# First block's attention: turning, copying and value products one step later, with a fourth buffer for the probabilities

## The chip, the cores and the metric

The kernel runs on one core of a Trainium2 chip. The time is device microseconds (us) of one launch. Five engines work beside each other, each through its own list of instructions in order: TensorE (PE; PEld is its weight load), VectorE (DVE), ScalarE (ACT), GpSimd (POOL) and SyncE (SP, which issues DMAs).

## The reference, cut to what matters

The program is a long chain: two layers of a first block (attention, a gated convolution network, an mLSTM layer, another network), then a second block. The change is in the attention of the first block's layer 0. There 768 tokens (512 of the sequence, 256 of a context) go through two attentions of 8 heads, and each is this:

```
def attend(q, k, v):                      # blocks of 128 queries
    s = einsum('bqgrd,bsgd->bgrqs', qi, k).astype(float32) * scale
    p = softmax(s, axis=-1)
    return einsum('bgrqs,bsgd->bqgrd', p, v)
...
ka, va = concatenate([ka_c, ka_l]), concatenate([va_c, va_l])   # context, sequence
out_lat = merge(attend(mla_q(...), ka, va), attend(gqa_q(...), kb, vb))
out_ctx = merge(attend(mla_q(ctx), ka_c, va_c), attend(gqa_q(ctx), kb_c, vb_c))
```

A block of sequence queries sees 768 keys; a block of context queries sees the 256 context keys. GQA has 8 query heads on 2 key heads; MLA has 8 heads of width 96.

## The kernel before, in words

All of it is written in fp32 with the operands of a large product split in a high and a low part (fp32r), so scores take two (GQA) or three (MLA) products.

`run()` inside `attn()` does an attention, once for GQA (178 to 283 us of the profile) and once for MLA (333 to 460 us). It cuts the work into 48 units: one head and one block t of 128 queries; t = 0 to 3 are of the sequence (768 keys wide), t = 4 and 5 of the context (256 wide). In MLA the units of a head follow each other (t0 to t5); in GQA two heads alternate, so twelve units make a group.

A unit goes through steps, each on one engine:

- `S`: scores, PE, into a double bank D of PSUM (two buffers).
- `X`: DVE finds the row maximum (L1938) and the bias (L1939); ACT writes exp and its row sum (L1942) into a buffer of the tag "ca" (three).
- `R`: DVE reciprocal (L1946), then POOL multiplies the probabilities (L1947).
- `Tr`: PE turns 128x128 pieces (L1958) into banks A (two buffers, columns up to 512) and B (one buffer, the last 256).
- `CpB` (ACT, L1963) and `CpA` (DVE, L1968): copies to SBUF, into one tile pT (four buffers).
- `PV`: at every odd unit PE multiplies the values with the pT of a pair of units (L1980: 24 matmuls, or 8 where the pair is 256 wide), into bank V (one buffer).
- `EvH` (ACT, L1995) and `EvL` (DVE, L2000): the high and low part of the output leave V.
- `preT`, `preH`, `preL`: the next head's queries and keys are turned on PE (three parts in MLA: two into a bank A at t0 and t1, the third into the D bank of unit t4), then split by ACT (L2014) and DVE (L2021).

`pipeline` sets the order. In round u it calls every step for unit u minus its lag, in the order of the list, and each engine executes what it is given in that order:

```
for u in range(n + max(l for l, _ in stages)):
    for lag, f in stages:
        if 0 <= u - lag < n:
            f(u - lag)
```

So one round is, on PE: S(u+1), preT(u), Tr(u-2), PV(u-4). On ACT: preH(u-1), CpB(u-3), exp(u), EvH(u-5). On DVE: maximum and bias (u), reciprocal (u-1), EvL(u-6), CpA(u-3), preL(u-1). On POOL: the product of u-1. Nothing is loaded from memory in either stage; a tail (`tail`) fills the rounds after the last unit.

A buffer that is taken again makes its first writer wait for its last reader. That is how an order on one engine becomes a wait on another.

Of the kernel before, what the change touches and what calls it, by code (L numbers as in the profile page):

```python
# [12 lines left out]
F32 = mybir.dt.float32  # L13
# [7 lines left out]
P = 128  # L21
# [4 lines left out]
TT = T + TC  # L26
# [155 lines left out]
class Kernel:  # L182
# [1503 lines left out]
    def attn(self):  # L1686
# [16 lines left out]
        esT, pT = self.pool("attT", "left")  # L1703
# [208 lines left out]
        def run(by_head, prep, scores, value, sc, out, bg, tail):  # L1912
# [4 lines left out]
            esW, pW = self.pool(self.nm("attW"), "left")  # L1917
            units = ([(h + c, t) for h in (0, 2, 4, 6) for t in range(6) for c in range(2)] if by_head else
                     [(h, t) for h in range(8) for t in range(6)])
            U = [dict(W=768 if t < 4 else 256) for h, t in units]  # L1920

            def S(u):
                h, t = units[u]
                d = U[u]
                d["s"] = b = self.bank("D").rearrange("p a b -> p (a b)")
                if t == 4 and h + by_head < 7:
                    U[u - 1]["pre"] = prep(h + 1 + by_head, 2, b[:, 0:512])
                if d["W"] == 768:
                    scores(h, t, b, 0, 512)
                scores(h, t, b, 512, 768)  # L1930

            def X(u):
                h, t = units[u]
                d = U[u]
                s = d.pop("s")[:, 768 - d["W"]:768]
                scale = sc[:, t, h:h + 1]
                mx, b = self.tmp(2, tag="mx", bufs=3), self.tmp(2, tag="mb", bufs=3)
                nc.vector.tensor_reduce(mx[:, 0:1], s, AX.X, ALU.max)  # L1938
                nc.vector.scalar_tensor_tensor(b[:, 0:1], mx[:, 0:1], -1.0, scale, ALU.mult, ALU.mult)  # L1939
                d["e"] = e = self.tmp(TT, tag="ca", bufs=3)[:, :d["W"]]  # L1940
                d["z"] = z = self.tmp(2, tag="z", bufs=6)
                nc.scalar.activation(e, s, AF.Exp, bias=b[:, 0:1], scale=scale, accum_out=z[:, 0:1])  # L1942

# [15 lines left out]

            def CpB(u):  # L1960
                d = U[u]
                d["p"] = p = pW.tile([P, TT], F32, tag="pT", bufs=4, name=self.nm("pT"))
                nc.scalar.activation(p[:, T:], d.pop("B")[:, :TC], AF.Copy)  # L1963

            def CpA(u):
# [57 lines left out]
            for i in range(6 if by_head else 3):  # L2023
                U[0]["pre"] = prep(i // 3, i % 3, self.bank("AAVBAA"[i]))
                preH(0)
                preL(0)
            S(0)
            self.pipeline(len(units), ((1, preH), (3, CpB), (0, X), (1, R), (6, EvL), (5, EvH), (3, CpA), (1, preL),
                                       (0, bg), (-1, S), (0, preT), (2, Tr), (4, PV)), tail)
            esW.close()  # L2030
            self.psum()

        def split_tile(pool, **kw):
            o = pool.tile([P, 2, 4, TT], F32R, name=self.nm("o"), **kw)
            return o[:, 0], o[:, 1]

        self.oG = split_tile(pO, tag="o")
        run(True, prep_g, scores_g, lambda h, j: G2[:, j, 128 + h // 4 * 64:192 + h // 4 * 64], scG, self.oG,
            kv_norm, lambda i: lat_q(i) if i < 2 else None)
        esg.close()  # L2040
# [87 lines left out]
        def tail(i):  # L2128
            if i == 0:
                self.ao_start()  # L2130
            if i < 4:
                self.ao_fm(self.ao0, self.w0, i)
        run(False, prep_m, scores_m, lambda h, j: V[:, j, h], scM,
            self.oM, lambda u: None, tail)
        esm.close()
# [639 lines left out]
```

## Time and profile before

| what | before |
|---|---|
| median of 3 runs | 3823.54 us (3820.2 to 3829.47) |
| profiled execution | 3818.78 us, of which 3817.0 us is its span |
| PE busy in the span | 3619.6 us, 95% |
| DVE, ACT, POOL busy | 67%, 42%, 19% |
| PE busy 178 to 286 us (GQA) | 95.85 of 108.00 us, granted clock 0.95 |
| PE busy 336 to 462 us (MLA) | 116.76 of 126.00 us, granted clock 0.96 |

The page gives averages over a program of many stages; the two stages here are 6% of the span, so they are read by themselves: PE's list in order of time, and what it waited for.

### The profile page before, as it was taken

To read this page: it belongs to the slowest core of one execution; us is meant where nothing else is said; L and a number is where in the kernel's file an instruction comes from. 1 tells how busy PE (TensorE), PEld (TensorE's weight loads), DVE (VectorE), ACT (ScalarE), POOL (GpSimd) and SP (SyncE) were. 2 spreads that over 40 slices of the span, in tenths; PEclk is the share of its full clock that TensorE was granted. 3 is DMA by queue.
4 is the path that set the end of the run, shared out by engine and by line. 5 is a ranking of instruction groups with operands and counts; after the bars stand their busy time and mean duration, and the time that the engine had idled before them with its cause. 6 is when DMAs were issued, how large, how long until landed. Compare 5 with 4: busy or idle time off the path is not lost. (4 is left out here: it accounts for less than half of the span.)

```text
span 3817.0 us, 54418 instructions
## 1 busy us (share of the span) xinstructions
PE 3619.6 (95%) x21148; PEld 3100.9 (81%) x21148; DVE 2564.8 (67%) x4103; ACT 1594.1 (42%) x2678; POOL 722.6 (19%) x755
## 2 busy tenths in 40 slices
PE   7988999999999989999999998999999999899999
PEld 5877788888887778877789876788878898678997
DVE  7977687665645285444577768677765777766776
ACT  2365632122235294332344446444444444464443
POOL 6334230010021193000100025000030000550000
PEclk8999999999999999999999998999999999899999
DMA  5300043343423542323233322333234332213332
GB/s 178 108 2 23 27 126 118 118 130 112 128 63 100 156 122 73 102 84 100 77 99 108 96 66 82 92 100 100 82 120 126 93 106 85 82 48 105 92 108 73
DMA packets 570400, 363.48 MB, mean 95 GB/s; under 512 B 17719, under 2 KB 546605, under 8 KB 570141
## 3 DMA queue, kind: packets, MB, share of 16 engines
q1 hardware_dynamic: 564317, 346.21, 31.1%
q0 software_dynamic: 3520, 9.59, 0.8%
q8 instruction: 167, 2.74, 0.3%
q10 hardware_dynamic: 2304, 4.20, 0.3%
q14 instruction: 92, 0.75, 0.1%
HBM read 345.72 MB, written 14.20 MB: 94 GB/s over the span
## 5 line engine op out<-in xcount | busy, mean ns | idle before, releaser
L135 DVE TENSOR_TENSOR wl<-ws,wh 128x1024 fp32r<-128x1024 f32 (+3 forms) x474 | 584.7, 1243 | 314.6 <-ACT wh L132 312.0
L132 ACT ACTIVATE wh<-ws 128x1024 fp32r<-128x1024 f32 (+3 forms) x474 | 457.6, 978 | 586.9 <-DVE ws L454 257.2
L562 PE MATMUL D<-ah,wl 128*128 128x256 f32 x1344 | 380.3, 283 | 11.0 <-DVE wl L135 11.0
L560 PE MATMUL D<-ah,wh 128*128 128x256 f32 x1344 | 377.1, 281 | 1.7 <-DVE gu L602 1.7
L561 PE MATMUL D<-al,wh 128*128 128x256 f32 x1344 | 376.5, 280 | 0.9 <-DVE al L495 0.9
L539 PE MATMUL M<-hz,wh 128*128 128x512 f32 x704 | 279.9, 398 | 2.3 <-DVE xT L545 2.3
L540 PE MATMUL M<-hz,wh 128*128 128x512 f32 x704 | 280.4, 398 | 1.0 <-DVE hz L638 0.9
L541 PE MATMUL M<-hz,wl 128*128 128x512 f32 x704 | 278.7, 396 | 0.0
L341 POOL TENSOR_TENSOR acc<-acc,t 128x512 f32<-128x512 f32 x36 | 46.8, 1301 | 1171.5 <-ACT t L340 1171.5
L562 PEld LDWEIGHTS D<-ah,wl 128*128 128x128 f32 x1344 | 252.7, 188 | 18.3 <-DVE wl L135 18.3
L560 PEld LDWEIGHTS D<-ah,wh 128*128 128x128 f32 x1344 | 252.8, 188 | 6.1 <-ACT wh L132 2.4
L561 PEld LDWEIGHTS D<-al,wh 128*128 128x128 f32 x1344 | 252.8, 188 | 5.0 <-DVE al L495 1.3
L321 PE MATMUL D<-ah,wl 128*128 128x512 f32 (+1 forms) x616 | 242.7, 394 | 6.5 <-DVE wl L135 6.5
L317 PE MATMUL D<-ah,wh 128*128 128x512 f32 (+1 forms) x616 | 244.7, 397 | 3.0 <-ACT wh L132 2.7
L319 PE MATMUL D<-al,wh 128*128 128x512 f32 (+1 forms) x616 | 242.8, 394 | 0.8 <-POOL al L2697 0.4
L303 POOL TENSOR_TENSOR hl<-t,hh 128x768 fp32r<-128x768 f32 (+1 forms) x44 | 69.9, 1588 | 796.4 <-ACT hh L302 735.9
L1349 DVE SCALAR_TENSOR_TENSOR as<-ws,S,as 128x256 f32<-128x256 f32 x448 | 202.8, 504 | 3.6 <-DMA ws<-in_ada_w_dram 0.2
L560 PE MATMUL E<-ah,wh 128*128 128x256 f32 x672 | 188.9, 281 | 6.8 <-ACT t L590 4.0
L562 PE MATMUL E<-ah,wl 128*128 128x256 f32 x672 | 189.9, 283 | 4.7 <-DVE wl L135 4.7
L561 PE MATMUL E<-al,wh 128*128 128x256 f32 x672 | 188.1, 280 | 0.0
L317 PE MATMUL D<-x7h,wh 128*128 128x512 f32 (+1 forms) x464 | 183.7, 399 | 2.6 <-ACT x7h L2692 1.6
L319 PE MATMUL D<-x7l,wh 128*128 128x512 f32 (+1 forms) x464 | 181.6, 394 | 0.6 <-DVE x7l L2699 0.6
(711 smaller groups left out, 9550.2 us busy)
## 6 DMA issues: line engine op xcount, KB each, us to landing
ws<-in_ffn_w_up_dram SPq DMA_DIRECT2D x104, 512.0 KB
ws<-in_ada_w_dram SPq DMA_DIRECT2D x88, 512.0 KB
t<-in_ffn_w_down_dram SPq DMA_DIRECT2D x128, 256.0 KB
ws<-in_ffn_w_gate_dram SPq DMA_DIRECT2D x88, 256.0 KB
ws<-in_ffn_w_up_dram SPq DMA_DIRECT2D x88, 256.0 KB
wz<-in_ffn_w_gate_dram SPq DMA_DIRECT2D x56, 256.0 KB
wz<-in_ffn_w_up_dram SPq DMA_DIRECT2D x56, 256.0 KB
ws<-in_ffn_w_down_dram SPq DMA_DIRECT2D x32, 384.0 KB
```

Of the source, the lines that this page charges most:

```text
L132: self.nc.scalar.activation(h[:, :n], t[:, :n], AF.Copy)
L135: self.nc.vector.tensor_tensor(l[:, :n], t[:, :n], h[:, :n], ALU.subtract)
L317: nc.tensor.matmul(o, wh[:, kw + k], xh[:, k0 + k, s], start=a, stop=False)
L319: nc.tensor.matmul(o, wh[:, kw + k], xl[:, k0 + k, s], start=False, stop=False)
L321: nc.tensor.matmul(o, wl[:, kw + k], xh[:, k0 + k, s], start=False, stop=z)
L539: nc.tensor.matmul(q, wh[:, k], h[:, 0, i], start=a, stop=False)
L540: nc.tensor.matmul(q, wh[:, k], h[:, 1, i], start=False, stop=False)
L541: nc.tensor.matmul(q, wl[:, k], h[:, 0, i], start=False, stop=z)
L560: nc.tensor.matmul(o, wh[:, u, k], xh(k0 + k, s), start=start and k == 0, stop=False, skip_group_check=True)
L561: nc.tensor.matmul(o, wh[:, u, k], xl(k0 + k, s), start=False, stop=False, skip_group_check=True)
L562: nc.tensor.matmul(o, wl[:, u, k], xh(k0 + k, s), start=False, stop=stop and k == 3, skip_group_check=True)
L1349: nc.vector.scalar_tensor_tensor(t, w[:, kk], c, t, ALU.mult, ALU.add)
```

## The change

The steps Tr, CpA, CpB, PV, EvH and EvL move one round later against S, X, R and the pre steps. The exp of every fourth unit goes to a buffer of its own in the stage's pool, so four units of probabilities can be held; the tiles pT go from four to three, so the SBUF used is the same.

```diff
-                d["e"] = e = self.tmp(TT, tag="ca", bufs=3)[:, :d["W"]]
+                e = (pW.tile([P, TT], F32, tag="e", name=self.nm("e")) if u % 4 == 3 else
+                     self.tmp(TT, tag="ca", bufs=3))
+                d["e"] = e = e[:, :d["W"]]
...
-                d["p"] = p = pW.tile([P, TT], F32, tag="pT", bufs=4, name=self.nm("pT"))
+                d["p"] = p = pW.tile([P, TT], F32, tag="pT", bufs=3, name=self.nm("pT"))
...
-            self.pipeline(len(units), ((1, preH), (3, CpB), (0, X), (1, R), (6, EvL), (5, EvH), (3, CpA), (1, preL),
-                                       (0, bg), (-1, S), (0, preT), (2, Tr), (4, PV)), tail)
+            self.pipeline(len(units), ((1, preH), (4, CpB), (0, X), (1, R), (7, EvL), (6, EvH), (4, CpA), (1, preL),
+                                       (0, bg), (-1, S), (0, preT), (3, Tr), (5, PV)), tail)
```

Lines after the new ones stand three lower in the changed kernel (L1942 becomes L1945, L1995 becomes L1998, L2014 becomes L2017). No instruction is added or removed on any engine, and the lists of the rest of the program are as before.

ACT's list in the MLA stage, rounds t2 to t5 of one head, before (mqh: the high part of the next head's queries and keys; pT<-B: a copy; t<-D: an exp; o<-V: an output):

```order
L1963 ACTIVATE pT_4347<-B_4330 128x256
L1942 ACTIVATE t_4353,t_4354<-D_4318,t_4350,scM 128x768
L1995 ACTIVATE o_3229<-V_4333 64x128 x2
L1963 ACTIVATE pT_4376<-B_4373 128x256
L1942 ACTIVATE t_4382,t_4383<-D_4361,t_4379,scM 128x768
L2014 ACTIVATE mqh_4294<-D_4390 96x2x256
L1963 ACTIVATE pT_4412<-B_4403 128x256
L1942 ACTIVATE t_4418,t_4419<-D_4390,t_4415,scM 128x256
L1995 ACTIVATE o_3229<-V_4406 64x128 x2
```

The same engine and rounds in the changed kernel:

```order
L1966 ACTIVATE pT_4536<-B_4532 128x256
L1945 ACTIVATE t_4542,t_4543<-D_4520,t_4539,scM 128x768
L1966 ACTIVATE pT_4573<-B_4557 128x256
L1945 ACTIVATE e_4579,t_4580<-D_4550,t_4576,scM 128x768
L1998 ACTIVATE o_3229<-V_4560 64x128 x2
L2017 ACTIVATE mqh_4477<-D_4586 96x2x256
L1966 ACTIVATE pT_4603<-B_4599 128x256
L1945 ACTIVATE t_4609,t_4610<-D_4586,t_4606,scM 128x256
```

EvH (o<-V) has moved from even rounds (after the exps of t2 and t4) to odd ones, and now stands between the exp of t3 and preH of the next head (mqh<-D).

DVE's list in the same stage, round t4 of one head, before (mql: the low part; D: a row maximum out of the scores):

```order
L1938 TENSOR_REDUCE t_4205<-D_4181 128x1
L1939 SCALAR_TENSOR_TENSOR t_4206<-t_4205,scM 128x1
L1946 RECIPROCAL t_4174<-t_4174 128x1
L1968 COPY pT_4203<-A_4189 128x512
L2021 TENSOR_TENSOR mql_4086<-D_4181,mqh_4085 96x2x256
```

And in the changed kernel:

```order
L1938 TENSOR_REDUCE t_4187<-D_4168 128x1
L1939 SCALAR_TENSOR_TENSOR t_4188<-t_4187,scM 128x1
L1949 RECIPROCAL t_4162<-t_4162 128x1
L2003 TENSOR_TENSOR o_3229<-V_4142,o_3229 64x128 x2
L1971 COPY pT_4185<-A_4176 128x512
L2024 TENSOR_TENSOR mql_4060<-D_4168,mqh_4059 96x2x256
```

EvL (o<-V,o) has moved into the rounds of even units, here between the reciprocal and the copy that stand ahead of the next head's preL (mql<-D).

## Rows read from the trace of the kernel before

**Rows 1.** Timeline of PE, one MLA head: start, duration, instruction, [idle before <- releaser].

```profile
400.72 1.53 PE L1980 MATMUL V<-pT,mv 128*64 128x128 f32 x24
402.18 0.50 PE L1908 MATMUL D<-mqh 96*128 96x512 f32 x1
...
403.34 0.60 PE L1958 MATMUL A<-ident,t 128*128 128x128 f32 x4
...
404.00 0.38 PE L1901 MATMUL D<-ident,mq 128*96 128x128 f32 x2
...
404.79 0.60 PE L1958 MATMUL A<-ident,t 128*128 128x128 f32 x4
...
405.54 0.66 PE L1980 MATMUL V<-pT,mv 128*64 128x128 f32 x8
406.13 0.39 PE L1908 MATMUL D<-mqh 96*128 96x256 f32 x1
...
407.03 0.38 PE L1958 MATMUL B<-ident,t 128*128 128x128 f32 x2
408.53 0.50 PE L1908 MATMUL D<-mqh 96*128 96x512 f32 x1 [1.11 <-DVE mql L2021]
```

**Rows 2.** Timeline of DVE in the same rounds.

```profile
403.54 0.96 DVE L1938 TENSOR_REDUCE t<-D 128x1 f32<-128x768 f32 x1 [0.80 <-PE D L1910]
...
404.80 0.59 DVE L2000 TENSOR_TENSOR o<-V,o 64x128 fp32r<-64x128 f32 x2
405.42 0.69 DVE L1968 COPY pT<-A 128x512 f32<-128x512 f32 x1
406.38 0.42 DVE L1938 TENSOR_REDUCE t<-D 128x1 f32<-128x256 f32 x1 [0.27 <-ACT mqh L2014]
...
406.99 0.67 DVE L1968 COPY pT<-A 128x512 f32<-128x512 f32 x1
407.78 0.69 DVE L2021 TENSOR_TENSOR mql<-D,mqh 96x512 fp32r<-96x512 f32 x1
```

**Rows 3.** Timeline of ACT in the same rounds.

```profile
404.79 0.99 ACT L1942 ACTIVATE t<-D,t,scM 128x768 f32<-128x768 f32 x1
...
405.77 0.58 ACT L2014 ACTIVATE mqh<-D 96x512 fp32r<-96x512 f32 x1
```

**Rows 4.** Waits, 349 to 463 us (MLA): us in total, times, longest.

```profile
PE D L1908 <- DVE mql L2021: 6.7, 6, 1.1
PEld A L1958 <- POOL t L1947: 0.7, 1, 0.7
```

**Rows 5.** Waits, 188.3 to 283.4 us (GQA).

```profile
PEld D L1888 <- ACT t L1942: 4.3, 11, 1.0
PE B L1958 <- ACT pT L1963: 2.4, 3, 0.9
PE A L1958 <- POOL t L1947: 1.7, 1, 1.7
```

**Rows 6.** Timeline of PE in GQA: one round, and a group's first scores twice.

```profile
216.06 0.50 PE L1888 MATMUL D<-gkh,qs 128*128 128x512 f32 x1
...
216.86 0.60 PE L1958 MATMUL A<-ident,t 128*128 128x128 f32 x4
...
217.61 1.53 PE L1980 MATMUL V<-pT,rawG 128*64 128x128 f32 x24
...
229.89 0.50 PE L1888 MATMUL D<-gkh,qs 128*128 128x512 f32 x1 [0.49 <-ACT t L1942]
...
254.90 0.48 PE L1888 MATMUL D<-gkh,qs 128*128 128x512 f32 x1
```

**Rows 7.** Timeline, end of MLA: an output that waits for its value product.

```profile
452.37 1.53 PE L1980 MATMUL V<-pT,mv 128*64 128x128 f32 x24
...
453.95 0.56 ACT L1995 ACTIVATE o<-V 64x128 fp32r<-64x128 f32 x2 [1.02 <-PE V L1980]
```

**Rows 8.** Busy us and counts by stretch: PE, PEld, DVE, ACT, POOL, PEclk, DMA.

```profile
328.00:349.00 21.00, 15.86 (x80) 12.66 (x79) 14.11 (x33) 10.60 (x23) 8.61 (x10) 0.83 0.00 1
```

## The prediction

> **What bounds the kernel now.** The page says that PE is busy 95% of the span, so I left the averages at once and read the two stretches in which the changed loop runs. First the waits of PE there, then the timelines of PE, DVE and ACT over one head. The reader is to see three things.
>
> In MLA, PE hardly waits for probabilities: one wait on POOL in the whole stage, 0.7 us [rows 4]. It waits once per head, for the low part of the next head's queries and keys, six times in the steady part, 6.7 us beyond the modelled ends of the matmuls [rows 4]. In the head shown, own work is at its end at about 407.18 (407.03 and the slot of two transposes, 0.15), and the next head's scores start at 408.53, released by mql [rows 1]: 1.35 us from start to start. The chain to it, counted from the end of S(t3) at 403.34, is: maximum of t3 at +0.20 [rows 2], its exp at +1.45, preH at +2.43 [rows 3], maximum of t4, which waits for preH, at +3.04, CpA at +3.65, preL at +4.44 [rows 2], scores at +5.19 [rows 1].
>
> In GQA, PE waits for many small things: for exp before scores 4.3 us in 11 waits, for the copy out of bank B 2.4, and once for POOL, 1.7 [rows 5]. A group of twelve units takes 254.90 - 229.89 = 25.01 us [rows 6].
>
> **The change part by part.** No instruction is added, so the price is only in waits. What the later Tr removes is the wait for POOL: 1.7 us in GQA and 0.7 in MLA [rows 4, 5], since a turn now stands a whole round behind the product that it needs. The fourth buffer costs nothing: it only keeps the exp of u+4 from waiting where u is held a round longer, and three buffers would otherwise have made it wait for the turn of the same round.
>
> Everything else that moves changes its parity. PV, which ran in odd rounds, runs in even ones; EvH goes from even to odd rounds, EvL from odd to even.
>
> *MLA.* I redo the chain above for the new order, origin again the end of S(t3).
> - DVE in round t2 now holds EvL besides the maximum and preL. From the start of a maximum to the next large operation 1.26 us, EvL 0.62 [rows 2], preL 0.69 by its busy time: 2.57. PE from the end of S(t2) to the end of S(t3): six transposes 0.66 and scores 1.16 [rows 1], 1.82. So the maximum of t3 starts at 0.20 + 2.57 - 1.82 = +0.95 (before +0.20).
> - exp(t3): +0.95 + 1.25 = +2.20. The copy CpB ahead of it on ACT must now wait, since with three pT tiles it takes the one that the previous round's PV reads. PV starts at about +0.22 (two transposes), ACT sees its end 453.95 - 452.37 = 1.58 later [rows 7], the copy takes 0.37 by an estimate from its width (half of the 768-wide exp's 0.99 and less [rows 3]): +2.17. Here this wait hides behind the maximum.
> - EvH now stands between that exp (0.98 to the next operation [rows 3]) and preH, 0.56 [rows 7]: preH at +3.74, maximum of t4 0.61 later at +4.35.
> - CpA 0.61 after the maximum [rows 2], but EvL's 0.62 is now ahead of it: +5.58; preL +6.27; scores 0.75 after preL starts [rows 1, 2]: +7.02.
> - PE's own work in the same stretch is now two transposes 0.22, PV 1.46, the pre part and S(t4) 0.79, Tr 0.66, S(t5) and Tr 1.05, a short PV 0.59 [rows 1]: 4.77. It stands 2.25 instead of 1.35: 0.90 more per head.
> - One wait is new. Tr of t3 into a bank A needs the CpA of t2, which now comes in round t0 behind a maximum and EvL: 0.20 + 1.26 + 0.62 + 0.69 = 2.77 after the end of S(t0) [rows 2], while PE needs Tr 0.66, S 1.16 and four transposes 0.44 [rows 1]: 0.51.
>
> That is 1.4 us per head; busy times count a little overlap twice (a 256-wide maximum occupies 0.61 before CpA starts, although its three operations last longer by their busy times), so I take 1.15. Ends: 0.3, if only EvH's place counts, and 1.6. With seven changes of head, +8.0 us (+2 to +11).
>
> *GQA.* I went through a group of twelve in the same way: S 0.80, Tr 0.66 to 0.75, PV 1.46 [rows 1, 6], 256-wide scores 0.32 by an estimate from their columns, two fifths of the 768-wide 0.80. PE's own work is 8 x 0.80 + 4 x 0.32 + 8 x 0.66 + 4 x 0.22 + 4 x 1.46 + 2 x 0.59 and 0.6 of pre parts = 21.5 of the 25.0 us, so it stands 3.5 before. After, the waits that I find are 0.6 in the round after the first PV (exp behind CpB behind PV, with preH ahead too), 0.5 at the same place after the next wide PV, 0.6 where EvL and the late maximum of the first narrow unit hold PV, and six of 0.1 to 0.2: about 2.7. So 0.8 less in each of three groups, and the 1.7 for POOL in the first: -4.1. The drain has one round more, in which the last PV has less to stand beside: +0.4. GQA -3.7; ends -14 (all four groups without a wait) and +6 (each wait of an exp counts 1.5 instead of 0.6).
>
> *Filling and draining MLA.* One Tr (0.66 [rows 1]) goes from a fill in which PE waits anyway to the end: +0.8, between 0 and 3. PE's clock is at 0.83 of full speed in the fill, 328 to 349 us [rows 8]; less work there may keep it at the lower of its two levels a while longer, which is in the upper end.
>
> Sum: 8.0 - 3.7 + 0.8 = +5.1 us on the profiled execution's 3818.78, 3823.9. The median of the runs shown lies 4.76 above that execution, so I expect 3828.6.
>
> One rule speaks for more than that. PE's gap in MLA is the same in every head [rows 1, 4], and its releaser is mql on DVE, no probabilities and no bank. The Trainium skill, page Perfetto Trace Analysis, section Identifying Performance Opportunities, says that the same gap repeating on the engine that should be saturated can mean too few buffers for the next tile. By that rule the fourth buffer would close the gap, and MLA would gain where the sum has a loss; the row's releaser speaks against it.
>
> **The rivals.**
> - *The gaps close.* The extra round takes all probabilities off PE's path, and what is left on DVE and ACT fits. MLA would gain 7 x 1.35 = 9.5, GQA some 9 of its 14: 3823.5 - 18.5 = 3805. For it: many small GQA waits on ACT [rows 5]. Against it: the MLA wait is on the pre steps [rows 4], which are not moved and get more work ahead of them. (This is also where the page's rule on buffers would lead.)
> - *The exp waits for PV (slower).* In every second round CpB waits for the PV of the round before, and the exp stands behind it on ACT. In a wide GQA pair the exp could start about 1.45 us after its scores (0.20 and 1.25 [rows 2, 3]), while PE does Tr 0.75, PV and 0.12 until ACT sees it, 2.3, and then the copy 0.3 comes: 1.15 late. If PE's other work covers only half of it, 0.6 x 32 wide pairs of both stages is +19 with nothing gained elsewhere: 3843. It decides from where the exp's end is later than PE's S and Tr after that PV (0.80 + 0.66 in GQA, 0.2 us short by my reckoning; 1.16 + 0.66 in MLA, no stall).
> - *Nothing to see.* PE's work in the two stretches is as before and the waits merely change places: 3823.5. For it: PE's busy share there.
>
> **How the numbers follow.** A change within 0.3% (11.5 us) is about what a measurement of this kernel can't tell from none. My forecast, a loss of 1 to 11 us: 0.55. Nothing to see or a small gain (to 11 us): 0.23. The gaps close, over 11.5 us gained: 0.08. The exp waits for PV, or the sum's upper ends together, over 11.5 lost: 0.14. So faster 0.08, same 0.78, slower 0.14. The range: 3814, which leaves out the larger gain, to 3842, where the upper ends of MLA and the fill (+14) and some GQA loss meet.
>
> **What would show it.** Right: in the MLA stage PE's wait for mql grows to about 2 us per head, EvH is seen just ahead of preH, a wait of PE for the copy out of A of about 0.5 appears in round t0; in GQA no wait for POOL, a group near 24.2 us; copies out of B on ACT that wait for V's matmuls every second round. Wrong: a wait for mql of 1.35 us or less per head (then DVE had more room in round t2 than I gave it), or exps in GQA that start later than 0.6 us behind their bias and hold scores in each pair, or a program outside the two stages that has become longer or shorter by more than a few us.

## The result, and the profile after

The changed kernel takes 3845.46 us (median of 4 runs, 3841.04 to 3849.86), the kernel before 3822.44 beside it: a ratio of 1.0062 [1.0051, 1.0074], 23 us slower. The profiled execution has a span of 3848.1 us.

The loss lies in the two stages. I measure each from its first scores to its last value product: GQA 106.27 us before and 111.02 after (+4.8), MLA 126.04 and 144.36 (+18.3). That is 23.1 together, as much as the medians differ. The two profiled spans differ by 31.1 us; the other 8.0 lie outside the stages, in code that did not change. Over the traces of all the runs here the time outside the stages goes from 3582 to 3595 us (3584.7 in the kernel before, 3592.7 in the changed one), so I read nothing from it.

PE over one MLA head after, which answers to [rows 1]. Columns: start, duration, engine, line, operation, tiles, size, count, [idle before <- releaser].

```profile
408.13 0.50 PE L1908 MATMUL D<-mqh 96*128 96x512 f32 x1 [0.66 <-DVE mql L2024]
...
412.07 0.63 PE L1961 MATMUL A<-ident,t 128*128 128x128 f32 x4 [0.48 <-DVE pT L1971]
...
417.04 0.28 PE L1910 MATMUL D<-mqh,mql 96*128 96x256 f32 x1
417.44 0.41 PE L1961 MATMUL B<-ident,e 128*128 128x128 f32 x2
417.77 1.53 PE L1983 MATMUL V<-pT,mv 128*64 128x128 f32 x24
...
422.27 0.44 PE L1961 MATMUL B<-ident,t 128*128 128x128 f32 x2 [0.40 <-ACT pT L1966]
423.35 0.66 PE L1983 MATMUL V<-pT,mv 128*64 128x128 f32 x8 [0.64 <-DVE o L2003]
424.80 0.54 PE L1908 MATMUL D<-mqh 96*128 96x512 f32 x1 [0.79 <-DVE mql L2024]
```

From first scores to first scores this head takes 16.67 us; before, every head from the third on took 14.78 (393.75 to 408.53 is one), and the first two 14.26 and 16.35. Where PE waited once at the end of a head, it now waits three times in a row: for the copy out of B, for EvL and for mql. The heads around it take 17.0 to 17.6.

DVE and ACT in the same rounds, for [rows 2, 3].

```profile
418.16 0.94 DVE L1938 TENSOR_REDUCE t<-D 128x1 f32<-128x768 f32 x1
...
421.99 0.42 DVE L1938 TENSOR_REDUCE t<-D 128x1 f32<-128x256 f32 x1 [2.62 <-ACT mqh L2017]
...
422.71 0.59 DVE L2003 TENSOR_TENSOR o<-V,o 64x128 fp32r<-64x128 f32 x2
423.33 0.69 DVE L1971 COPY pT<-A 128x512 f32<-128x512 f32 x1
424.06 0.69 DVE L2024 TENSOR_TENSOR mql<-D,mqh 96x512 fp32r<-96x512 f32 x1
```

```profile
419.40 0.39 ACT L1966 ACTIVATE pT<-B 128x256 f32<-128x256 f32 x1 [1.13 <-PE V L1983]
419.68 0.99 ACT L1945 ACTIVATE e<-D,t,scM 128x768 f32<-128x768 f32 x1
...
420.78 0.55 ACT L1998 ACTIVATE o<-V 64x128 fp32r<-64x128 f32 x2
421.36 0.59 ACT L2017 ACTIVATE mqh<-D 96x512 fp32r<-96x512 f32 x1
```

Counted from the end of S(t3) at 417.16 (the start of its last matmul, 417.04, and 0.12), the chain is: maximum of t3 at +1.00, exp at +2.52, preH at +4.20, maximum of t4 at +4.83, CpA at +6.17, preL at +6.90, scores at +7.64. The steps stand in the order that I had worked out, each 0.05 to 0.63 later. This is one of the long chains: from head to head they alternate between about 7.6 and 7.1 us, which I had not foreseen.

Waits of MLA (357 to 489 us), for [rows 4], and of GQA (178 to 292), for [rows 5]: us in total, times, longest.

```profile
ACT pT L1966 <- PE V L1983: 30.4, 23, 3.3
DVE t L1938 <- ACT mqh L2017: 15.3, 6, 2.6
PE D L1908 <- DVE mql L2024: 4.3, 6, 0.8
PE V L1983 <- DVE o L2003: 3.4, 6, 0.6
PE B L1961 <- ACT pT L1966: 2.2, 7, 0.4
```

```profile
ACT pT L1966 <- PE V L1983: 22.1, 18, 2.1
PE D L1888 <- ACT t L1945: 5.6, 12, 1.3
PE B L1961 <- ACT pT L1966: 1.5, 3, 0.6
```

PE's wait for mql got shorter in this view, 6.7 to 4.3 us, while the head got longer: a wait view shows only the last wait of an instruction, and part of the time now ends on two earlier ones. New are the copies out of B that wait for the value product.

The first scores of the third GQA group and of the fourth, for [rows 6]: 25.31 us apart instead of 25.01.

```profile
234.16 0.50 PE L1888 MATMUL D<-gkh,qs 128*128 128x512 f32 x1
...
259.47 0.50 PE L1888 MATMUL D<-gkh,qs 128*128 128x512 f32 x1
```

Stretches after: MLA's fill, for [rows 8], then two heads and two pieces at a change of head. Columns: stretch, its length, busy us (instructions) of PE, PEld, DVE, ACT, POOL, granted clock of PE (1.00 is 2.4 GHz, 0.50 is 1.2), DMA share, GB/s.

```profile
336.00:357.00 21.00, 15.31 (x74) 12.02 (x73) 13.57 (x32) 9.79 (x21) 8.65 (x9) 0.83 0.00 1
...
408.10:424.80 16.70, 14.24 (x127) 11.80 (x127) 12.07 (x32) 10.57 (x27) 4.60 (x6) 1.00 0.01 1
424.80:441.80 17.00, 15.61 (x126) 13.24 (x126) 11.88 (x32) 10.46 (x27) 4.62 (x6) 0.90 0.01 1
...
421.30:424.80 3.50, 1.67 (x17) 0.95 (x15) 2.67 (x8) 1.94 (x6) 0.91 (x1) 1.00 0.00 0
424.80:428.80 4.00, 4.00 (x15) 3.62 (x16) 2.91 (x10) 1.79 (x6) 0.96 (x2) 0.57 0.00 0
```

The second and the third head before, in the same columns:

```profile
349.00:364.20 15.20, 14.09 (x124) 12.28 (x123) 10.17 (x26) 9.70 (x26) 4.15 (x6) 0.90 0.00 1
364.20:379.00 14.80, 13.69 (x127) 11.90 (x127) 11.96 (x32) 10.62 (x28) 4.58 (x6) 1.00 0.01 2
```

The fill's clock is as before, 0.83, and the second head has 0.90 in both kernels. New is the clock from the third head on: 0.90 in all but one, where every head before had 1.00. After 3.5 us in which PE did 1.67 us of work, it is at 0.57 for the next 4 us, mostly on the lower of its two levels; about the same 126 matmuls are busy 15.6 us instead of 14.2 over the head.

### The profile page after: what moved, and what is told of

Read it like the earlier page. It is cut to its first block, busy times and chain, and to the rows that moved or that the text cites. A ratio compares the mean times of both kernels' runs of the same rounds, so it can differ in the third digit from the quotient of the medians.

```text
span 3848.1 us, 54413 instructions
## 1 busy us (share of the span) xinstructions
PE 3640.5 (95%) x21148; PEld 3112.5 (81%) x21148; DVE 2568.5 (67%) x4103; ACT 1592.1 (41%) x2678; POOL 724.8 (19%) x755
## 3 DMA queue, kind: packets, MB, share of 16 engines
q0 software_dynamic: 3520, 9.59, 0.9%
```

## The experiments

Of each run I read the ratio to the kernel before, the stages, and five MLA heads (the third to the seventh), parted into the stretch from their first scores to the end of S(t3), in which PE has most of the work, and the chain from there to the next head's scores. All of it comes from the starts in PE's timeline.

| run | ratio [95%] | GQA us | head = stretch + chain | clock in these heads |
|---|---|---|---|---|
| before | | 106.3 | 14.78 = 9.59 + 5.19 | 1.00 |
| changed | 1.0062 [1.0051, 1.0074] | 111.0 | 17.22 = 9.80 + 7.42 | 0.90, one 1.00 |
| gqa_only | 1.0014 [1.0005, 1.0022] | 111.2 | 14.78 = 9.59 + 5.18 | 1.00 |
| mla_only | 1.0043 [1.0030, 1.0056] | 106.3 | 17.47 = 10.06 + 7.41 | 0.83 to 1.00 |
| before_pt3 | 1.0017 [1.0008, 1.0026] | 110.7 | 14.79 = 9.60 + 5.18 | 1.00 |
| after_pv4 | 1.0038 [1.0025, 1.0050] | 108.7 | 15.90 = 10.72 + 5.18 | 1.00 |
| before_pv5 | 1.0058 [1.0045, 1.0071] | 109.8 | 17.13 = 9.52 + 7.61 | 0.90 |
| pv5_free | 1.0009 [1.0000, 1.0018] | 105.9 | 15.38 = 8.25 + 7.13 | 1.00, one 0.90 |
| pv5_free_evl | 1.0015 [1.0007, 1.0024] | 110.1 | 14.98 = 7.94 + 7.04 | 1.00 |
| after_pb4 | 1.0044 [1.0032, 1.0057] | 106.2 | 17.09 = 9.96 + 7.13 | 0.90 |
| after_pb4_fill | 1.0033 [1.0020, 1.0045] | 107.7 | 16.22 = 9.09 + 7.13 | 1.00 |
| after_pb4_evl | 1.0033 [1.0021, 1.0044] | 110.0 | 15.53 = 9.43 + 6.11 | 1.00 |
| after_fill2 | 1.0050 [1.0037, 1.0062] | 111.2 | 16.50 = 9.08 + 7.42 | 1.00 |
| after_x | 1.0087 [1.0073, 1.0101] | 126.6 | 16.68 = 9.09 + 7.59 | 1.00 |
| after_ev | 1.0077 [1.0064, 1.0089] | 113.5 | 17.72 = 9.78 + 7.94 | 0.85 to 1.00 |

**Which stage.** The lags, the buffer and the tile count were made to depend on the stage.

```diff
+            k = int(by_head)     # mla_only: int(not by_head)
-  (3, CpB) ... (6, EvL), (5, EvH), (3, CpA) ... (2, Tr), (4, PV)
+  (3 + k, CpB) ... (6 + k, EvL), (5 + k, EvH), (3 + k, CpA) ... (2 + k, Tr), (4 + k, PV)
```

> The later turns, copies and products with three pT tiles and the fourth buffer, in the GQA stage alone; MLA keeps the order of before. Theory 1 (the head change of MLA carries the loss, because EvH and EvL now stand in its chain): MLA heads are 14.8 us again at full clock, the GQA stage keeps its +6 us of the profile, so the kernel is about 6 us above the kernel before, ratio 1.0010 to 1.0025. Rival (the loss is general, each exp waiting for the product in both stages): more than half of the loss stays, ratio 1.0035 or more. If the GQA stage by itself does not lose, the ratio is 1.000.

> The reverse: the change in MLA alone, GQA as before. Theory 1: heads of 16.7 to 17.6 us, PE's granted clock at its lower level once in most heads, the kernel 16 to 20 us above the kernel before, ratio 1.0042 to 1.0052. Rival (general loss, half in each stage): ratio below 1.0035 and a head under 16 us.

Both came out as the first theory had it, but for one MLA head of 18.5 us: +5.2 and +16.5 us by the medians, which make up nearly the whole. The two stages are separate questions.

These traces also show how far a stage of equal code can differ. MLA is the same in the kernel before and in gqa_only, but takes 126.0 and 123.3 us: the first two heads together take 30.6 and 28.0, the second at a granted clock of 0.90 and 1.00. A difference in the first two heads alone therefore says little.

**GQA: the wait of the copy.** The order of before with three tiles:

```diff
-  tag="pT", bufs=4
+  tag="pT", bufs=3
```

> The order of before with three pT tiles instead of four, nothing else. It sets the wait of the copy out of B (and of the exp behind it on ACT) for the product of the round before, without the change of parity. Theory 2 (that wait carries the loss): ratio 1.004 or more, and MLA heads of 16 us or more. Theory 1 (the place of EvH and EvL carries it): MLA heads of 14.8 to 15.1 us, GQA at most 3 us longer, ratio 0.9995 to 1.0015. Both together: in between.

In GQA this alone costs 4.4 us, more than the 3 that theory 1 allowed and nearly the change's 4.8; the third group takes 25.99 us (232.63 to 258.62). From its waits (178 to 290 us):

```profile
ACT pT L1963 <- PE V L1980: 27.5, 22, 1.9
```

In MLA it costs the heads nothing (14.79), as theory 1 had it: there something else makes the loss. The reverse, the later steps in GQA with four tiles (gqa_only with `bufs=4`):

> As gqa_only (the later steps in the GQA stage alone, MLA as before), but with four pT tiles again beside the fourth buffer of the probabilities, so that no copy out of B waits there for the product of the round before. Theory (that wait is what GQA loses, as the order of before with three tiles already showed with 110.7 us for the stage): stage 105.5 to 107.5 us instead of 111.2, ratio to before 0.9990 to 1.0005. Rival (the loss is the longer fill and the later turns): stage 109 us or more, ratio 1.0010 or more.

The stage fell to 107.6, just above the theory's 107.5, and the third group to 24.45. The ratio, 1.0015 [1.0006, 1.0024], did not follow: the median of eleven runs stayed 6 us above the kernel before, of which the stage shows 1.4. I can't place the rest. The GQA stage of equal code, too, differs between profiles: it takes 106.2 us in after_pb4 and 107.7 in after_pb4_fill below, all of it in the first group (25.92 us at a granted clock of 0.93, 27.43 at 0.81; the first group before has 0.80, that of gqa_pt4 0.81). Putting the exp ahead of the copy in the list instead was a miss:

```diff
-  ((1, preH), (4, CpB), (0, X), (1, R), (7, EvL)
+  ((1, preH), (0, X), (1, R), (4, CpB), (7, EvL)
```

> The changed kernel with the maximum and exp of a round ahead of its copy out of B in the list, so that the exp on ACT no longer stands behind a copy that waits for the product of the round before. Theory (exp behind that copy is what lengthens the chain at the head change beyond what I had worked out, and the GQA groups too): GQA stage 2 to 4 us shorter than the 111.0 of the changed kernel, heads of MLA 0.3 to 0.5 us shorter at full clock, fewer stretches at the lower clock, ratio to before 1.0030 to 1.0048. Rival (the copy is then later by the exp's 0.9 us, the turns into B wait for it, and PE stands as long as now): ratio 1.0055 or more.

The rival held in GQA, whose stage grew to 126.6 us: bank B is single, so the next turn waits for the copy wherever the copy stands. Its waits of PE (178 to 308 us), against 1.5 in three times in the changed kernel:

```profile
PE B L1961 <- ACT pT L1966: 12.0, 17, 1.2
```

In MLA the heads fell to 16.7 us at a clock of 1.00, but the chain did not get shorter.

**MLA: which of the moved steps.** The change cut in two: turns and copies late, products as before (after_pv4), and the reverse (before_pv5).

```diff
   after_pv4, against the changed kernel
-  (7, EvL), (6, EvH) ... (3, Tr), (5, PV)
+  (6, EvL), (5, EvH) ... (3, Tr), (4, PV)
   before_pv5, against the kernel before
-  (6, EvL), (5, EvH) ... (2, Tr), (4, PV)
+  (7, EvL), (6, EvH) ... (2, Tr), (5, PV)
```

> The changed kernel with the products, and what follows them, one step earlier again (PV 4, EvH 5, EvL 6 steps behind the scores): turns and copies stay later, the rounds of PV, EvH and EvL are those of before, and no copy out of B takes a pT tile that the product of the round before reads. Theory (the loss is the changed parity in MLA and the wait for that product in GQA): MLA heads of 14.8 to 15.2 us at full clock, GQA stage 105 to 107 us, ratio 0.9985 to 1.0010. Rival (later turns and copies cost by themselves, since the product now stands behind the copies of its own round): heads of 16 us or more, ratio above 1.0030.

> The kernel before with PV, EvH and EvL one step later and turns and copies where they were; the other half of the change beside the run that had the products early and the turns late (heads of 15.9 us, ratio 1.0038). The pT tiles are four, and with the later product a copy out of B again takes the tile that the product of the round before reads. If the two halves add up (1.1 us per head from the turns, 0.7 from the products, 0.6 from the clock): heads of 15.4 to 15.6 us, ratio 1.0010 to 1.0030. If the later product is the worse half by itself (EvH and EvL in the chain, exp behind the copy): heads of 16 us and more, stretches at the lower clock, ratio 1.0035 or more. If the products only cost on top of late turns: heads of 14.8 us, ratio below 1.0010.

The halves don't add up, and the theory of after_pv4 was a miss. Late turns cost 1.1 us per head and leave the chain at 5.18: a wide turn has moved ahead of S(t3), and a pre part waits for a bank A (345 to 450 us):

```profile
PE A L1898 <- DVE pT L1971: 2.7, 6, 0.5
```

Late products alone cost 2.35, nearly the whole: the chain grows to 7.61, as PV, EvH and EvL enter it, and the clock falls in every head.

**The wait of the copy apart from EvH and EvL.** The tile pT was parted, its 256 columns out of B (pB) in five tiles, its 512 out of A (pA) in four and only for wide units. In this order no copy then waits for a product in MLA.

```diff
-  d["p"] = p = pW.tile([P, TT], F32, tag="pT", bufs=4, ...)
+  pA = pW.tile([P, T], F32, tag="pA", bufs=5 if by_head else 4, ...) if d["W"] == 768 else None
+  pB = pW.tile([P, TC], F32, tag="pB", bufs=5, ...)
```

> As before_pv5 (products, EvH and EvL one step later, turns and copies where they were), with the pT tile parted in two: its 256 columns for the copy out of B in five tiles, its 512 for the copy out of A in four (five in GQA) and only for wide units. In MLA no copy then takes a tile that the product of the round before reads. Theory A (EvH, 0.57 us, and EvL, twice 0.6, in the chain of the head change carry most of it): heads of 16.5 to 17.1 us, the lower clock stays in most heads, ratio 1.0040 to 1.0058. Theory B (the copy that waits for the product, with the exp behind it, carries most): heads of 15.6 us or less, clock 1.00, ratio 1.0030 or less.

> As pv5_free, and EvL moved to the end of DVE's work in the round in which EvH is, so that it stands neither ahead of the maximum of t3 nor ahead of CpA and preL of round t4; EvH stays where it is. Theory A: 1.2 us less in the chain, heads of 15.2 to 15.7 us, clock 1.00, ratio 1.0005 to 1.0020. Theory B: as pv5_free, within 0.2 us per head.

```diff
   pv5_free_evl, against pv5_free
-  (7, EvL), (6, EvH), (3, CpA), (1, preL),
+  (6, EvH), (3, CpA), (1, preL), (6, EvL),
```

The first run's numbers are those of theory B, but the chain tells how: it fell by 0.48 only, 7.61 to 7.13. The larger part, 1.27, is the stretch, where the clock came back: 7.9 us in the four heads at 1.00, and in the one head at 0.90 the 9.52 of before_pv5 again.

```profile
381.50:396.30 14.80, 13.60 (x127) 11.82 (x127) 11.80 (x32) 10.51 (x27) 4.59 (x6) 1.00 0.01 2
396.30:411.50 15.20, 13.66 (x126) 11.77 (x126) 11.88 (x32) 10.62 (x27) 4.59 (x6) 1.00 0.01 2
411.50:427.90 16.40, 15.19 (x127) 13.19 (x127) 11.87 (x32) 10.47 (x27) 4.59 (x6) 0.90 0.00 1
```

One head of five still drops, and is 1.1 to 1.6 us longer than its neighbours. Moving EvL brought 0.4 us more per head, but 0.3 of that is the one dropped head, which no longer drops; the chain is 0.09 shorter, where theory A asked for 1.2. At equal clock this is the side of theory B, within 0.2 us per head. It lost in GQA (110.1 us), where EvL at that place waits for EvH (17.6 us in 22 waits instead of 6.1 in 4). The same parting in the changed kernel, with one tile of each kind fewer:

> The changed kernel with the pT tile parted in the same way, the part for the copy out of B in four tiles, the part for the copy out of A in three in MLA and four in GQA. The copy out of B and the exp behind it then wait for no product of the round before, and the exp needn't be moved. Theory A: heads of MLA at most 0.5 us shorter, GQA stage 107 to 108 us, ratio to before 1.0040 to 1.0055. Theory B: heads of 15.9 us or less, clock 1.00, ratio 1.0030 or less.

Here theory B fails: GQA is back at 106.2 us with a third group of 24.46, but the heads are 17.09 and the clock 0.90. With no wait of a copy out of B (those out of A still wait for a product in MLA, 6.4 us in 8 waits), the chain has nearly the numbers of the prediction (S(t3) ends at 407.35; again one of the long chains, 7.35 against 6.82 in the heads between):

```profile
409.58 0.99 ACT L1945 ACTIVATE e<-D,t,scM 128x768 f32<-128x768 f32 x1 [1.12 <-DVE t L1949]
...
411.26 0.59 ACT L2020 ACTIVATE mqh<-D 96x512 fp32r<-96x512 f32 x1
```

```profile
411.89 0.42 DVE L1938 TENSOR_REDUCE t<-D 128x1 f32<-128x256 f32 x1 [2.33 <-ACT mqh L2020]
...
413.24 0.69 DVE L1974 COPY pA<-A 128x512 f32<-128x512 f32 x1
413.96 0.69 DVE L2027 TENSOR_TENSOR mql<-D,mqh 96x512 fp32r<-96x512 f32 x1
```

Exp +2.23 (worked +2.20), preH +3.91 (+3.74), maximum +4.54 (+4.35), CpA +5.89 (+5.58), preL +6.61 (+6.27), scores +7.35 (+7.02). EvL moved as above, in this kernel:

> As after_pb4 (the changed kernel, no copy waits for the product of the round before), and EvL at the end of DVE's work in EvH's round. In after_pb4 the chain of the head change stands at 7.35 us from the end of the scores of t3 (7.02 worked out, 7.64 in the changed kernel), so in MLA EvH and EvL are what is left of it. If so: chain of about 6.2 us, heads of 15.7 to 16.2 us at full clock, clock 0.95 or more, ratio to before 1.0018 to 1.0035. Rival (another wait has the same length, as the turn into a bank A that waits for CpA): chain 6.9 us or more, heads of 16.7 us or more, ratio 1.0038 or more.

As expected: chains of 5.9 to 6.4 at a clock of 1.00, with heads of 15.53, a little under what was expected. GQA loses again by EvL's new place (110.0). From the maximum of t4 to preL it is 1.40 again, as in [rows 2], instead of 2.07:

```profile
409.72 0.42 DVE L1938 TENSOR_REDUCE t<-D 128x1 f32<-128x256 f32 x1
...
410.33 0.67 DVE L1974 COPY pA<-A 128x512 f32<-128x512 f32 x1
411.12 0.69 DVE L2027 TENSOR_TENSOR mql<-D,mqh 96x512 fp32r<-96x512 f32 x1
```

With the same aim, but on the changed kernel with its waiting copies, EvH was put behind preH and EvL behind preL, both in even rounds:

> The changed kernel with EvH moved behind preH and EvL behind preL in the list (EvH one step later, so both in even rounds); parity of PV, pT tiles and e buffers stay as changed. Theory 1 (EvH's 0.56 and EvL's 0.62 us in the chain of the head change are what lengthens the head, and the lower clock follows from the longer gap): heads of 15.3 to 15.8 us, no or fewer stretches at the lower clock, 8 to 12 us less than the changed kernel, ratio to before 1.0030 to 1.0042. Rival (the wait of the copy out of B for the product sets the chain, EvH and EvL stand in its shadow): heads of 16.5 us or more, ratio 1.0055 or more.

The rival's side, and worse. V has one buffer, and the later EvL held the short product that stands ahead of the scores in PE's queue (355 to 470 us):

```profile
PE V L1983 <- DVE o L2003: 8.3, 6, 1.4
```

**The clock.** Twelve turns more per head, to keep PE busy: first ahead of the new head's scores, in their bank (after_fill), then behind t1's turns into A, repeated (after_fill2, after_pb4_fill). They write what is overwritten, or the same again.

```diff
   after_fill, in S
+  if not by_head and t == 0 and h:
+      for j in range(12): nc.tensor.transpose(b[:, 0:P], self.ident, self.ident)
   after_fill2, after_pb4_fill, in Tr
+  if not by_head and units[u][1] == 1 and j == 3:
+      for k in range(12): nc.tensor.transpose(d["A"][:, k % 4 * P:][:, :P], e[:, k % 4 * P:][:, :P], self.ident)
```

> The changed kernel with twelve more 128x128 turns on PE in MLA ahead of the first scores of each new head, whose output the scores overwrite: PE works instead of standing there. Theory 3 (PE's gap at the head change brings the granted clock down, and that lengthens the head a second time): no stretch at the lower level between heads, heads of 16.7 us throughout, 3 to 5 us less than the changed kernel, ratio to before 1.0050 or less. Rival (the clock level costs nothing, since the chain on ACT and DVE sets the head): clock 1.00 but heads still 17.2, same time. If the turns wait for the bank and then hold the scores up, up to 9 us more than the changed kernel.

1.0069 [1.0056, 1.0081] with heads of 18.4 us, a miss: the bank comes free only with preL, so the turns stood behind the gap.

> The changed kernel with the four turns of t1's block into bank A done four times over in MLA (twelve more turns per head, 1.3 us, same output into the same bank), where PE would stand before the turns into B, the product and the next head's scores. It fills a part of the gap without a wait of its own. Theory 3 (the gap brings the granted clock down, and the lower level lengthens the head a second time): no stretch at the lower level, heads of 16.7 to 16.9 us, 2 to 4 us less than the changed kernel, ratio to before 1.0050 to 1.0057. Rival (the level costs nothing since the chain over ACT and DVE sets the head): clock 1.00, heads still 17.2, same time. If the gap left is still enough for the lower level: as the changed kernel or up to 2 us more.

> As after_pb4, with t1's four turns into bank A done four times over in MLA (twelve more turns per head, same output), to hold the clock. If the clock is what lies between the heads of 17.1 us there and the 15.3 of the run that has the same chain of 7.35 us at full clock: heads of 15.8 to 16.3 us, clock 1.00, 5 to 8 us less than after_pb4, ratio to before 1.0022 to 1.0032. Rival (the later turns lengthen the head by themselves, at either level): clock 1.00, heads of 16.5 us or more, ratio 1.0035 or more.

Both held in the heads, at the same chain; the ratio of after_pb4_fill lies just above the expected 1.0032. The five heads together are 3.6 and 4.4 us shorter. The MLA stage is 136.6 us instead of 144.4, and 134.4 instead of 138.7; 2.3 us of the first difference are in the first two heads. The ratios fell by 0.0012 and 0.0011, some 4 us, with intervals that overlap those of the kernels without the turns; the verdict rests on the profiles, one trace of each. Stretches of after_fill2, and one of after_pb4_fill:

```profile
382.90:386.40 3.50, 2.72 (x28) 2.28 (x26) 2.69 (x8) 1.92 (x6) 0.91 (x1) 1.00 0.01 2
...
402.60:419.30 16.70, 15.29 (x139) 13.11 (x139) 12.07 (x32) 10.69 (x28) 4.59 (x6) 1.00 0.01 1
```

```profile
384.20:400.20 16.00, 14.96 (x139) 13.13 (x139) 11.88 (x32) 10.62 (x27) 4.58 (x6) 1.00 0.01 3
```

The Trainium skill, page Perfetto Trace Analysis, section Matmul Optimizations, says that the matmul engine scales its power with its use, so that products should come back to back. These runs agree as far as the granted clock tells it: 0.90 without the turns, 1.00 with them.

**Is there something to gain in the kernel before?** Its gap of 1.35 us per head, tried from two sides.

```diff
   before_preA: the third pre part turned into a bank A in round t2
-  if t == 4 and h + by_head < 7:        (S)      if t < 2 and h < 7:   (preT)
+  if by_head and t == 4 and h < 6:      (S)      if t < 3 and h < 7:   (preT)
   before_preL
-  (3, CpA), (1, preL),
+  (1, preL), (3, CpA),
```

> The kernel before, with the third pre part of a head in MLA turned into a bank A in round t2, as the first two are in t0 and t1, instead of into the scores' bank of t4. The scores of the next head then wait neither for preL of round t4 nor for the release of that bank. If the chain through preH, the maximum of t4, CpA and preL is the whole gap of 1.35 us, seven of them go: heads of 13.5 to 13.7 us, 8 to 10 us less, ratio 0.9975. Rival (another chain is right behind it: the free D bank behind the exp of t4, or the turns of t2 behind the third user of the two banks A): heads of 14.4 us or more, ratio 0.9990 to 1.0020.

> The kernel before with preL ahead of CpA in the list, nothing else. In MLA the chain at the head change then has preL 0.6 us earlier. If that chain is the whole gap of 1.35 us: heads of 14.2 us, 4 us less, ratio 0.9985 to 0.9995. Rival (the copy out of A, now 0.7 us later, is waited for by a turn or a product, as the turned pre part in a bank A was): heads of 14.6 us or more, ratio 0.9995 to 1.0015.

No measurable gain: 1.0003 [0.9994, 1.0012] and 1.0005 [0.9996, 1.0013], heads of 14.83 and 14.79. With a third user of the banks A, a turn waits for CpA where the scores waited for mql; with preL first, preL waits for the exp of t4, which reads the same bank D. One row of each (345 to 450 us):

```profile
PE A L1958 <- DVE pT L1968: 7.5, 6, 1.3
```

```profile
DVE mql L2021 <- ACT t L1942: 5.0, 7, 0.7
```

No run was faster than the kernel before.

## Why the prediction was wrong

It put +5.1 us where there are 23, outside its range (3814 to 3842). Three steps failed. The sum had no term for PE's clock after the longer gaps in MLA. It took the wait of the copy for hidden in MLA. And in GQA it booked a gain of 4.1 us that did not come. By terms:

- **MLA, heads: +8.0 predicted, +12.9 measured** (the seven periods from first scores to first scores make 117.4 us against 104.5). The mechanism was right: EvH ahead of preH, EvL ahead of CpA, the turn of t3 behind CpA (412.07, 0.48 idle). The worked order gives a stretch of 9.08 (9.59, less a PV of 1.46, and 0.44 for a wide turn and 0.51 for the wait) and a chain of 7.02; after_fill2 has 9.08 and 7.42. So at full clock 1.3 to 1.4 were worked out, 1.7 is there, and I had then cut it to 1.15 for an overlap that these runs don't show. Of the 0.4 in the chain, 0.29 is the copy that waits for PV (7.42 to 7.13), "hidden behind the maximum" in the prediction: its PV stands behind a turn that waits for the copy before it. The other 0.72 per head (17.22 to 16.50) is PE's clock. The sum had no term for it: I looked at the clock in the fill alone, where nothing changed.
- **How the heads' 2.44 divide**, by the runs in a row: clock 0.72, the copy's wait 0.28 (16.50 to 16.22), EvL 0.69 (16.22 to 15.53), and 0.75 left for EvH and the later turns, which no run here parts. The shares go by this order of the runs and are not costs by themselves: late turns alone cost 1.12 in after_pv4.
- **MLA, fill and drain: +0.8 predicted, +5.4 measured** for the last head with the drain (26.96 against 21.54 us). In after_fill2 it is 25.05, in after_pb4_fill 23.91: some 1.9 is the clock again, 1.1 the copy, the rest the longer drain.
- **MLA together.** With the clock held and no wait of the copy out of B (after_pb4_fill) the stage is 8.4 us longer than before, where I had summed 8.8. That the two agree is in part luck: the five steady heads are 7.2 longer, not 5.8, and the first two 1.2 shorter, because the profile of the kernel before has its second head at the lower clock.
- **GQA: -3.7 predicted, +4.8 measured**, the largest single error, 8.5 us. By groups I had -2.5, -0.8, -0.8 and +0.4 for the last with its drain; measured are +1.2, +0.4, +0.3 and +2.9. The step that failed is the gain. The wait for POOL in the first group is gone, as worked, but the start had no term: with the turns a round later, the first turn comes 10.4 us after the first scores instead of 7.6, and one more scores product waits for an exp ahead of it:

```profile
188.49 0.80 PE L1888 MATMUL D<-gkh,qs 128*128 128x512 f32 x1 [1.33 <-ACT t L1945]
```

  The room in a group was too large as well: I summed 21.5 us of PE's own work, but the third group before has PE busy for 22.26 of its 25.01 us:

```profile
229.89:254.90 25.01, 22.26 (x214) 18.91 (x215) 19.92 (x54) 18.17 (x47) 9.16 (x12) 1.00 0.01 2
```

  The wait of the copies was not mis-sized in sum: I had 0.6 and 0.5 in each of three groups, 3.3 us, and taking it away saves 3.6 (gqa_only 111.2, gqa_pt4 107.6), half of that in the last group with its drain. Without it my terms would give -7.0, and gqa_pt4 has +1.4. How the start, the room and the longer drain share that difference no run here parts.
- **The rival "the exp waits for PV"**, which I had at 0.14 together with the upper ends, has its waits in both stages. What they cost is 3.6 us in GQA and some 2.5 in MLA's five heads and drain (five times 0.28, and 1.1), not the 19 of that rival.
- **"The fourth buffer costs nothing"**: no run here has that buffer by itself. What paid for it, the third pT tile less, costs GQA those 3.6 us.
- **The page's rule** (a repeating gap can mean too few buffers; the Trainium skill, page Perfetto Trace Analysis, section Identifying Performance Opportunities): with the fourth buffer of probabilities MLA's gap did not close, as the releaser in [rows 4] had said, though the later steps came with it. Of the copies' tiles the rule held, once the products came late: with more tiles the heads of before_pv5 go from 17.13 to 15.38.

What I announced as a sign, a wait for mql of 2 us per head, wasn't seen (0.8): the time sat in three waits, and only the distance between first scores showed it. Of the other signs, the wait for the copy out of A (0.48), EvH ahead of preH and the end of the wait for POOL came; the group of 24.2 did not (25.31). The 8.0 us outside the two stages would be a sign of being wrong, but they lie within the 13 us over which the traces of these runs spread there.

## What to carry to other kernels

Moving a step by one round in a pipeline whose units pair up moves its evacuations into the other parity of rounds: look which chain they join there, and measure the distance between equal landmarks, not one wait. When a buffer is paid for with another, ask which writer now waits for which reader, and what is queued behind that writer. Give the start of a pipeline a term of its own: a longer lag adds a round in which the busiest engine has only the first step to do. And give a longer gap on PE a second price: work after it may run at the lower clock.

## What the runs showed of the hardware that I had not expected

- Adding 1.3 us of turns to each head shortened the head from 17.22 to 16.50 us on average, the granted clock being 1.00 in place of 0.90.
- The price of one drop of the clock differs with the order of the work: 1.6 us in a head of pv5_free (16.34 against 14.74), 0.9 in one of the changed kernel (17.60 against 16.67), each beside a head with the same chain. Why it differs no run here shows.
- Gaps of nearly one size can end on either level: in pv5_free the clock stayed at 1.00 after a gap in one head and fell to 0.57 after one in another. PE was busy 1.97 and 1.96 us in the 3.5 us ahead.

```profile
378.00:381.50 3.50, 1.97 (x18) 1.25 (x16) 2.64 (x8) 1.86 (x6) 0.91 (x1) 1.00 0.01 2
...
408.00:411.50 3.50, 1.96 (x18) 1.24 (x16) 2.63 (x8) 1.87 (x6) 0.91 (x1) 1.00 0.00 0
411.50:415.50 4.00, 3.96 (x15) 3.53 (x16) 2.89 (x9) 1.69 (x6) 0.93 (x2) 0.57 0.00 0
```
